# Moving columns of four up tile pairs and two down tiles in other orders

## The chip, the cores and the metric

One core of a Trainium2 chip runs the kernel. The metric is the device time of one execution in microseconds (us); 1108.68 us is the median of three runs before the change.

## The reference

The kernel computes one encoder block for 256 tokens and 16 meta tokens (`L` = 272) of width 2048 in float32: attention by two groups of heads, an output projection, and a gated MLP. The change lies in the MLP alone:

```python
def conv_glu(x, w_gate, w_up, conv_w, conv_b, w_down):
    g = x @ w_gate
    u = x @ w_up
    ...
    gc = conv_b
    for i in range(CONV_W):
        gc = gc + conv_w[i] * gp[:, i:i + L]
    return (jax.nn.silu(gc) * u) @ w_down
```

`w_gate` and `w_up` are 2048 x 5632, `w_down` is 5632 x 2048. The meta tokens are dropped at the end, so up and down need 256 tokens only.

## The kernel before

**Numbers.** Each float32 operand is split in two parts, high and low, of a type that TensorE takes faster than plain float32 (`F32R`): ScalarE writes the high part (L238), VectorE the difference (L242). A product is then three matmuls, high x high, high x low, low x high (`mm3`, L603 to L609; its matmuls are L606, L607 and L608). Weights stand still in the array as blocks of 128 x 128; activations are the moving operand, with the tokens as its columns. So one matmul writes 128 output features x 256 (or 258, or 272) tokens into a bank, and the sums over the blocks of the contraction collect in the bank.

**Weights.** Weights come from memory in pieces of up to 1024 columns (`raw`), are split into `whi` and `wlo`, and are consumed block by block: `block()` (L583) waits until a piece is split and `used()` (L590) steps on.

**Activations of the MLP.** `hl` (L629) holds the normed input, 16 blocks of 128 features, each with a high and a low half of 272 columns. `act` (L1735) holds the gated values, 44 blocks, each with a high and a low half of 256 columns that lie one behind the other, 512 columns in a row.

**Up.** The 44 tiles of 128 columns of `w_up` stand in 22 pairs. Twelve pairs (six groups of four tiles from the list `QUADS`, L48) go through another scheme with fewer products (`scheme_products`, L1924). The other ten, pairs 0, 1, 4, 7, 10, 13, 16, 17, 20 and 21, are direct: `mm_up` (L1874) calls `mm3` for each of 16 blocks and both tiles, 96 matmuls of 256 columns in a pair, into the first 256 columns of two banks. After the last block VectorE multiplies the bank with the gate (`tile_up`, L1775).

**Down.** Of the 16 tiles of `w_down`, eight go through the scheme and eight are direct. For seven of the direct ones `mm2` (L1866) is used: one matmul takes the high weights against both halves of `act` at once, 512 columns into the whole bank (L1870), and a second takes the low weights against the high half, 256 columns into the first half of the bank (L1871). `down_out` (L1842) adds the two halves of the bank. The last direct tile uses `mm3`.

**What sets the order.** The program is written by a planner (`Flow`, L111): each helper yields an engine and a cost, and the planner, with a clock for each engine, picks what can start first (`run`, L187). For an up block the cost is three times 0.445 x columns + 3 ns, for a block of `mm2` 347 ns. TensorE's order in the MLP is the list `work` (L427 on): gate and up pairs with the pieces of the scheme between them, and then down tiles with pieces of the scheme between them. `mlp_weights` (L1878) walks that list: `which` is the number of the pair or of the down tile, `k` the block in an up pair, `f` the block in a down tile.

## Time and profile before

| | |
|---|---|
| median of three runs | 1108.68 us (1108.24 to 1108.7) |
| span of the profiled execution | 1106.7 us |
| time of the profiled execution beside its span | not recorded apart; the median of the runs is 2.0 us above the span |
| instructions | 22544, of them 8414 matmuls |
| TensorE busy | 1100.6 us |
| VectorE busy | 990.8 us |
| ScalarE busy | 735.1 us |
| the four up pairs | near 390, 413, 478 and 544 us |
| the two down tiles | 871.6 to 926.7 us, with pieces of the scheme between |

The span runs from the first to the last instruction. In the groups of instructions "bank<-hl,whi 128\*128 128x256" is a matmul that reads the moving tile `hl` and the weights `whi`, 128 x 128 weights, 256 columns. Matmuls overlap, so that the durations of their records sum to more than the time they take; the distance from one start to the next is what one costs.

### The profile page before, as it was taken

What the parts mean: (1) busy time and instruction counts of PE and PEld (TensorE: products, weight loads), DVE (VectorE), ACT (ScalarE), POOL (GpSimd) and SP (SyncE); (2) the same over time, 40 slices, a digit from 0 to 9 for tenths busy, and PEclk for the clock granted to TensorE, in tenths of its full rate; (3) what the DMA queues carried; (4) which work ended last, traced back from release to release, by engine and by line L of the source; (5) the groups of instructions that cost most, each with busy time, mean ns of one, the idle gap of its engine ahead of it and who ended that gap; (6) DMA issues with size and microseconds to landing.
All of it is one profiled execution on the core that took longest, in us unless ns stands there. A gap on an engine that the chain in (4) does not pass through costs nothing.

```text
span 1106.7 us, 22544 instructions
## 1 busy us (share of the span) xinstructions
PE 1100.6 (99%) x8414; PEld 1061.8 (96%) x8414; DVE 990.8 (90%) x1837; ACT 735.1 (66%) x1470; POOL 140.0 (13%) x202
## 2 busy tenths in 40 slices
PE   9999999999999999999999999999999999999998
PEld 9999999999999999999999999999999988888888
DVE  8979888888878989999999999988988999999984
ACT  8788979798647776656666565665565565655663
POOL 3211222121433400000000000000000011100114
PEclk9999999999999999999999999999999999999999
DMA  9553434444665796657667577777688787777772
GB/s 323 199 172 124 148 127 151 139 163 134 230 188 161 207 343 229 198 181 243 224 193 230 179 248 241 238 229 244 203 275 299 260 299 250 251 258 266 281 249 77
DMA packets 72374, 239.41 MB, mean 216 GB/s; under 512 B 8136, under 2 KB 12744, under 8 KB 72264
## 3 DMA queue, kind: packets, MB, share of 16 engines
q1 hardware_dynamic: 71976, 237.69, 63.8%
q8 instruction: 66, 1.08, 0.4%
q14 instruction: 44, 0.36, 0.1%
q10 hardware_dynamic: 288, 0.27, 0.1%
HBM read 219.44 MB, written 17.83 MB: 214 GB/s over the span
## 4 chain that ended last, share of the span: by engine, by line
PE 90%; ACT 4%; DVE 3%; issue 1%; DMA 1%; POOL 0%; DVEq 0%; POOLq 0%; ACTq 0%
PE bank L278 24%; PE bank L606 18%; PE bank L607 18%; PE bank L608 18%; PE bank L1870 6%; PE bank L1871 3%; PE bank L284 2%; ACT whi L238 1%; ACT scr L238 1%; DVE wlo L242 1%; DVE scr L250 1%; DMA raw<-in_w_cq 1%; ACT qraw L238 0%; ACT bank L238 0%; DVE cols L258 0%
## 5 line engine op out<-in xcount | busy, mean ns | idle before, releaser
L238 ACT ACTIVATE whi<-raw 128x512 fp32r<-128x512 f32 (+2 forms) x479 | 358.1, 764 | 173.2 <-PE bank L607 83.5
L242 DVE TENSOR_TENSOR wlo<-raw,whi 128x512 fp32r<-128x512 f32 (+2 forms) x479 | 414.9, 885 | 43.2 <-ACT whi L238 42.1
L606 PE MATMUL bank<-hl,whi 128*128 128x258 f32 (+2 forms) x1528 | 438.5, 287 | 0.1
L607 PE MATMUL bank<-hl,whi 128*128 128x258 f32 (+2 forms) x1528 | 433.7, 284 | 0.0
L608 PE MATMUL bank<-hl,wlo 128*128 128x258 f32 (+2 forms) x1528 | 433.0, 283 | 0.2 <-DVE wlo L242 0.2
L608 PEld LDWEIGHTS bank<-hl,wlo 128*128 128x128 f32 x1528 | 290.1, 190 | 0.9 <-DVE wlo L242 0.7
L607 PEld LDWEIGHTS bank<-hl,whi 128*128 128x128 f32 x1528 | 289.6, 190 | 0.1
L606 PEld LDWEIGHTS bank<-hl,whi 128*128 128x128 f32 x1528 | 288.6, 189 | 0.5 <-ACT scr L238 0.3
L238 ACT ACTIVATE whi<-quarters 128x1024 fp32r<-128x1024 f32 x88 | 81.5, 950 | 64.8 <-PE bank L1870 46.0
L278 PE MATMUL bank<-whi,act 128*128 128x256 f32 (+1 forms) x420 | 111.5, 317 | 0.0
L1870 PE MATMUL bank<-act,whi 128*128 128x512 f32 x308 | 110.1, 397 | 0.0
L242 DVE TENSOR_TENSOR wlo<-quarters,whi 128x1024 fp32r<-128x1024 f32 x88 | 99.4, 1156 | 10.8 <-ACT whi L238 10.2
L266 POOL TENSOR_TENSOR mt<-mt,mt 128x256 f32<-128x256 f32 x7 | 6.8, 979 | 652.4 <-ACT mt L238 652.4
L1871 PE MATMUL bank<-act,wlo 128*128 128x256 f32 x308 | 86.4, 281 | 0.0
L278 PE MATMUL bank<-whi,sin 128*128 128x512 f32 (+1 forms) x272 | 83.5, 355 | 0.0
L278 PEld LDWEIGHTS bank<-whi,act 128*128 128x128 f32 x420 | 74.1, 189 | 5.7
L1870 PEld LDWEIGHTS bank<-act,whi 128*128 128x128 f32 x308 | 57.8, 188 | 13.9
L278 PE MATMUL bank<-whi,hl 128*128 128x256 f32 x288 | 66.5, 280 | 0.0
L278 PE MATMUL bank<-wlo,act 128*128 128x256 f32 (+1 forms) x210 | 66.3, 315 | 0.0
L238 ACT ACTIVATE whi<-more_raw 128x1024 fp32r<-128x1024 f32 (+2 forms) x46 | 44.1, 962 | 24.4 <-PE bank L607 9.9
L1871 PEld LDWEIGHTS bank<-act,wlo 128*128 128x128 f32 x308 | 58.1, 189 | 1.6
L278 PEld LDWEIGHTS bank<-whi,sin 128*128 128x128 f32 x272 | 49.5, 188 | 7.7
(278 smaller groups left out, 1947.9 us busy)
## 6 DMA issues: line engine op xcount, KB each, us to landing
raw<-in_w_gate SPq DMA_DIRECT2D x83, 512.0 KB, 5.0
raw<-in_w_in SPq DMA_DIRECT2D x52, 512.0 KB, 3.9
raw<-in_w_up_s SPq DMA_DIRECT2D x44, 512.0 KB, 4.9
quarters<-in_w_down_s SPq DMA_DIRECT2D x44, 512.0 KB, 6.9
raw<-in_w_up SPq DMA_DIRECT2D x34, 512.0 KB, 5.5
raw<-in_w_out SPq DMA_DIRECT2D x32, 512.0 KB, 4.0
raw<-in_w_down SPq DMA_DIRECT2D x32, 512.0 KB, 5.2
s_down<-sums SPq DMA_DIRECT2D x22, 512.0 KB, 4.1
```

The source lines that it names most:

```text
L238: nc.scalar.activation(out, in_, f, **kw)
L242: nc.vector.tensor_tensor(out, a, b, op)
L250: nc.vector.scalar_tensor_tensor(out, a, s, b, op0, op1)
L266: nc.gpsimd.tensor_tensor(out, a, b, op)
L278: nc.tensor.matmul(o, l, r, start=start, stop=stop)
L284: nc.tensor.transpose(o, i, ident[:n, :n])
L606: nc.tensor.matmul(ps, whi, xhi, start=start, stop=False)
L607: nc.tensor.matmul(ps, whi, xlo, start=False, stop=False)
L608: nc.tensor.matmul(ps, wlo, xhi, start=False, stop=stop)
L1870: nc.tensor.matmul(ps, whi, x, start=start, stop=False)
L1871: nc.tensor.matmul(ps[:, :n], wlo, x[:, 0, :], start=False, stop=stop)
```

## The change

Some matmuls read their moving columns, and write the bank, in another order. The order is a number from 0 to 7: 0 is the plain one, 7 is backwards, and 1 to 6 take runs of 2, 4, 8, 16, 32 or 64 columns in turn from the first and the second half of the columns. Source and bank take the same order, so each column still lands in its place.

In the direct up pairs with a number below 8 (0, 1, 4 and 7) the order is the block number modulo 8, for all three products. In the down tiles 0 and 1 it is the block number modulo 7, for the matmul of 512 columns alone: there the two halves are the high and the low half of `act`.

```diff
-    def mm2(ps, x, n, start, stop):
+    def mm2(ps, x, n, start, stop, order):
 
         whi, wlo = yield from block()
         yield "pe", 347
-        nc.tensor.matmul(ps, whi, x, start=start, stop=False)
+        both = x
+        if order:
+            both = x.rearrange("p i (c e) -> p c i e", e=1 << order)
+        nc.tensor.matmul(ordered(ps, order), whi, both, start=start, stop=False)
         nc.tensor.matmul(ps[:, :n], wlo, x[:, 0, :], start=False, stop=stop)
         used()
 
-    def mm_up(ps, k):
-        h = (hl[k][:, i, :SEQ] for i in range(2))
-        yield from mm3(ps[:, :SEQ], *h, k == 0, k == KC - 1)
+    def ordered(t, k):
+        if k == 0:
+            return t
+        if k == 7:
+            return t[:, ::-1]
+        e = 1 << k
+        return t.rearrange("p (h c e) -> p c h e", h=2, e=e)
+
+    def mm_up(ps, k, order):
+        h = (ordered(hl[k][:, i, :SEQ], order) for i in range(2))
+        yield from mm3(ordered(ps[:, :SEQ], order), *h, k == 0, k == KC - 1)
...
-                        yield from (mm_gate if kind == "gate" else mm_up)(pss[c], k)
+                        if kind == "gate":
+                            yield from mm_gate(pss[c], k)
+                        else:
+                            yield from mm_up(pss[c], k, k % 8 if which < 8 else 0)
...
-                        yield from mm2(ps, act[:, f], SEQ, f == 0, f == FC - 1)
+                        yield from mm2(
+                            ps, act[:, f], SEQ, f == 0, f == FC - 1, f % 7 if which < 2 else 0
+                        )
```

## The prediction

> **What bounds the kernel now.** I read the page's busy times, slices and chain first, then the waits of TensorE, then windows over the stretches that the change touches. Of the page:

> ```profile
> span 1106.7 us, 22544 instructions
> ...
> PE 1100.6 (99%) x8414; PEld 1061.8 (96%) x8414; DVE 990.8 (90%) x1837; ACT 735.1 (66%) x1470; POOL 140.0 (13%) x202
> ...
> PE   9999999999999999999999999999999999999998
> ...
> PEclk9999999999999999999999999999999999999999
> ...
> PE 90%; ACT 4%; DVE 3%; issue 1%; DMA 1%; POOL 0%; DVEq 0%; POOLq 0%; ACTq 0%
> PE bank L278 24%; PE bank L606 18%; PE bank L607 18%; PE bank L608 18%; PE bank L1870 6%; PE bank L1871 3%; PE bank L284 2%; ACT whi L238 1%; ACT scr L238 1%; DVE wlo L242 1%; DVE scr L250 1%; DMA raw<-in_w_cq 1%; ACT qraw L238 0%; ACT bank L238 0%; DVE cols L258 0%
> ```

> TensorE is busy 1100.6 of 1106.7 us at the full granted clock, and 90% of the chain that ended last is its matmuls. A busy matmul row alone does not prove that the engine is never held up, so the second view is what TensorE waited for, all of it:

> ```profile
> PE bank L698 <- DVE em L695: 1.1, 1, 1.1
> PE bank L278 <- POOL sq8r L266: 0.5, 2, 0.3
> PE bank L608 <- DVE wlo L242: 0.2, 1, 0.2
> ```

> That is 1.8 us in the whole execution. The windows over two of the four up pairs (413 and 482) and two stretches of the two down tiles (871.6 and 926.5) show the same there:

> ```profile
> core 0: us, PE busy (x) PEld busy (x) DVE busy (x) ACT busy (x) POOL busy (x), PEclk, DMA share, GB/s
> ...
> 413.00:424.00 11.00, 11.00 (x96) 11.00 (x95) 9.78 (x19) 8.17 (x14) 0.00 (x0) 1.00 0.69 235
> 482.00:490.00 8.00, 8.00 (x70) 8.00 (x69) 7.60 (x14) 3.44 (x4) 0.00 (x0) 1.00 0.45 145
> ...
> 871.60:880.00 8.40, 8.40 (x49) 7.28 (x49) 8.40 (x18) 3.77 (x6) 0.00 (x0) 1.00 0.87 302
> ...
> 926.50:930.00 3.50, 3.50 (x18) 2.90 (x17) 3.17 (x4) 3.28 (x6) 1.34 (x2) 1.00 1.01 370
> ```

> VectorE is close behind (8.40 of 8.40 us in the first down tile), but nobody on TensorE waits for it. So a nanosecond added to a matmul here is a nanosecond of the span: there is no idle time to swallow it, and the work that could have hidden it (the splits on ScalarE and VectorE, the weight loads) is work that waits for TensorE, not the other way round.

> **What a matmul costs in the stream.** The duration of a record (about 280 ns for 256 columns) is not its cost, since matmuls overlap. The cost is the step from one start to the next. The second up pair, 96 matmuls (16 blocks, 2 tiles, 3 products) and the first one behind it:

> ```profile
> 412.98 0.28 PE L606 MATMUL bank<-hl,whi 128*128 128x256 f32 x1
> ...
> 424.23 0.28 PE L608 MATMUL bank<-hl,wlo 128*128 128x256 f32 x1
> 424.34 0.28 PE L606 MATMUL bank<-hl,whi 128*128 128x258 f32 x1
> ```

> (424.34 − 412.98) / 96 = 118.3 ns for 256 columns. The first 24 blocks of the first down tile, each a matmul of 512 columns and one of 256, and then nine matmuls of 512 columns of the scheme:

> ```profile
> 871.55 0.39 PE L1870 MATMUL bank<-act,whi 128*128 128x512 f32 x1
> 871.78 0.28 PE L1871 MATMUL bank<-act,wlo 128*128 128x256 f32 x1
> ...
> 880.03 0.40 PE L278 MATMUL bank<-whi,sin 128*128 128x512 f32 x1
> ...
> 882.11 0.39 PE L1870 MATMUL bank<-act,whi 128*128 128x512 f32 x1
> ```

> A block takes (880.03 − 871.55) / 24 = 353 ns, so its wide half takes 353 − 118 = 235 ns; the nine take 2.08 / 9 = 231 ns each. From 231.1 and 118.3 follows a slope of 112.8 / 256 = **0.44 ns per column** and some 5.5 ns per instruction that do not depend on the columns.

> **The change part by part.** No instruction, wait, DMA or semaphore is added, removed or moved: the planner's costs (351 ns for the three products of an up block, 347 ns for a down block) are what they were, so it writes the same order, and no queue (SP's and POOL's included) is passed by anything. What changes is only the order in which some matmuls read their moving columns and write their bank. The groups that hold them:

> ```profile
> L1870 PE MATMUL bank<-act,whi 128*128 128x512 f32 x308 | 110.1, 397 | 0.0
> L606 PE MATMUL bank<-hl,whi 128*128 128x256 f32 x320 | 90.7, 283 | 0.0
> L607 PE MATMUL bank<-hl,whi 128*128 128x256 f32 x320 | 90.0, 281 | 0.0
> L608 PE MATMUL bank<-hl,wlo 128*128 128x256 f32 x320 | 89.8, 281 | 0.0
> ```

> Up: pairs 0, 1, 4 and 7 are the direct ones below 8, so 4 × 96 = 384 of the 960. The order is the block number modulo 8: 48 matmuls stay plain, and each of the orders 1 to 6 (runs of 2, 4, 8, 16, 32, 64 taken in turn from the two halves of 128 columns) and 7 (backwards) has 4 × 2 × 2 × 3 = 48. That is 336 altered matmuls of 256 columns. Down: two tiles of 44 blocks, order the block number modulo 7; order 1 comes 7 times in a tile and orders 2 to 6 six times each, so 14 and 5 × 12, in all 74 altered matmuls of 512 columns, which take runs in turn from the high and the low halves. The narrow matmul behind each (L1871) stays as it is.

> Loads of the stationary operand keep their addresses and are hidden as now. The instruction's fixed share stays at 5.5 ns. The unknown is the column: what it costs when its neighbour in time is not its neighbour in the buffers. The trace before has no such matmul, so I bound it. Below: two matmuls of one form with other addresses already differ in step,

> ```profile
> 482.26 0.29 PE L607 MATMUL bank<-hl,whi 128*128 128x256 f32 x1
> 482.39 0.28 PE L608 MATMUL bank<-hl,wlo 128*128 128x256 f32 x1
> ...
> 482.87 0.28 PE L606 MATMUL bank<-hl,whi 128*128 128x256 f32 x1
> 482.98 0.28 PE L607 MATMUL bank<-hl,whi 128*128 128x256 f32 x1
> ```

> 0.13 us in the first pair of rows and 0.11 in the second. If every altered matmul came down from the mean to that lower step, it would gain some 8 ns, and as much twice over where it is wide: 336 × 8 + 74 × 16 = 3.9 us gained at most. Above: the slower streams that the trace does have are the transposes and the plain float32 matmuls at the start,

> ```profile
> 489.97 1.04 PE L284 MATMUL bank<-ident,raw 128*128 128x128 f32 x8
> ...
> L284 PE MATMUL bank<-ident,raw x48: 270/273/273, 490.0 to 864.0; 128*128 128x128 f32 x48
> ...
> 1.05 3.35 PE L698 MATMUL bank<-em 128*128 128x128 f32 x14 [1.05 <-DVE em L695]
> ...
> L698 PE MATMUL bank<-em x14: 421/421/579, 1.1 to 4.0; 128*128 128x128 f32 x14
> ```

> Eight transposes take (1.04 − 0.27) / 7 = 110 ns per 128 columns, 0.86 ns a column, close to twice 0.44; fourteen plain matmuls take (3.35 − 0.42) / 13 = 225 ns, 1.76 ns a column. A stream that cannot keep its pace thus falls to about half of it or to a quarter; half is the nearest row, and I take it as the price of an order that the buffers cannot serve.

> Which orders are those? A matmul's end is already a jump, to another source tile and another bank, and costs at most those 5.5 ns. Runs of 64 make 4 such jumps in 256 columns; at 5.5 ns they would be 22 ns, at one lost column 2 ns. Runs of 2 make 128 of them, and there is no time in 0.88 ns per run for anything to be caught up. So the price should sit on the shortest runs, and I take it in two ways. At half pace for runs of 2 alone: 48 × 256 × 0.44 + 14 × 512 × 0.44 = 5.4 + 3.2 = 8.6 us. At one lost column for each run, in all orders: 48 × (128 + 64 + 32 + 16 + 8 + 4) + 14 × 256 + 12 × (128 + 64 + 32 + 16 + 8) = 18,656 runs × 0.44 ns = 8.2 us. Both come to **+8.4 us**, though they spread it differently over the orders.

> [...]

> The profiled execution's span is 1106.7 us and the median of the runs is 1108.68; the 2.0 us around the span have no part in the change. Forecast: 1108.7 + 8.4 = **1117.1 us**.

> **The rivals.** *No order costs anything:* the pairs in a run of 2 are served at pace, backwards too, or the patterns reach the engine as what they were. For it speaks that every instruction's jump is nearly free now. 1108.7 us. *Only backwards is slow:* two neighbours are always together except that they come the wrong way round, so 48 × 113 ns = 5.4 us, 1114.1 us; runs of 2 keep pace in this case. *Both are slow:* 8.6 + 5.4 = 14 us, 1122.7 us. *Every altered order falls to half pace:* 336 × 113 ns + 74 × 226 ns = 38.0 + 16.7 = 54.7 us, 1163.4 us; against it speaks that runs of 64 have so few jumps. By the quarter pace of the plain matmuls it would even be 336 × 338 ns + 74 × 676 ns = 164 us, 1272 us, which I leave out. *Faster:* the uneven steps quoted above come from addresses that collide, and reading from two places in turn avoids it. With two thirds of the bound, 2.6 us, the time is 1106.1 us. It decides from a mean gain of 5.4 ns on the 410 altered matmuls (2.2 us); the rows give no hint that order rather than address sets the step.

> **How the numbers follow.** Forecast 0.33, no cost 0.25, backwards alone 0.14, both 0.12, all at half pace 0.09, faster 0.07. About 0.2% (2.2 us) is what a measurement of this kernel can tell from no change. So slower is 0.33 + 0.14 + 0.12 + 0.09 = 0.68, same 0.25, faster 0.07. A range from 1106.5 to 1124 us holds the first four, 0.84, and leaves out the faster case and the half pace of all orders.

> **What would show it.** In the profile after, the steps in an up pair tell every order apart, since the order changes with each six matmuls: plain blocks should step at 118 ns, runs of 2 at about 230 (half pace) or 175 (lost columns, with 147 at runs of 4 and 133 at runs of 8), backwards at 118. The four pairs should then grow from 11.4 us by 1.35 us each, or by 1.3 with the loss spread. In the down tiles the wide step should be about 460 ns in one block of seven. The prediction is wrong if blocks with long runs slow as much as short ones, if backwards moves at all, or if no step moves. It is wrong in its first part if the steps grow and the span does not, which would need TensorE to have had time to spare.

## The result and the profile after

The changed kernel takes 1114.24 us (1113.76 to 1114.38) against 1108.69 us before in the same series: a ratio of 1.005 with a 95% interval of 1.0034 to 1.0066, 5.55 us more. The forecast was 8.4 us more.

The page and TensorE's waits after the change:

```profile
span 1111.9 us, 22544 instructions
...
PE 1106.0 (99%) x8414; PEld 1065.5 (96%) x8414; DVE 990.8 (89%) x1837; ACT 736.1 (66%) x1470; POOL 140.6 (13%) x202
...
PE 92%; ACT 3%; DVE 3%; issue 1%; POOL 0%; DVEq 0%; POOLq 0%; ACTq 0%
```

```profile
PE bank L698 <- DVE em L695: 1.1, 1, 1.1
PE bank L278 <- POOL sq8r L266: 0.5, 2, 0.3
```

The span has grown by 5.2 us and TensorE's busy time by 5.4 us, with the same instructions and no new wait; VectorE's busy time is what it was. So the time went into the matmuls. Which ones is read from the timeline. These are the first matmuls of blocks 1, 2, 3, 4, 7 and 8 of the second up pair; six matmuls lie from one block to the next, so a sixth of the distance is the step:

```profile
414.30 0.33 PE L606 MATMUL bank<-hl,whi 128*128 128x256 f32 x1
...
415.29 0.30 PE L606 MATMUL bank<-hl,whi 128*128 128x256 f32 x1
...
416.08 0.29 PE L606 MATMUL bank<-hl,whi 128*128 128x256 f32 x1
...
416.82 0.28 PE L606 MATMUL bank<-hl,whi 128*128 128x256 f32 x1
...
418.97 0.28 PE L606 MATMUL bank<-hl,whi 128*128 128x256 f32 x1
...
419.68 0.28 PE L606 MATMUL bank<-hl,whi 128*128 128x256 f32 x1
```

Runs of 2 (block 1) step at 0.99 / 6 = 165 ns, runs of 4 at 132, runs of 8 at 123, and the three blocks from 16 to 64 with (418.97 − 416.82) / 18 = 119 ns are where plain blocks are. Backwards (block 7) has 118 ns. In the first down tile, blocks 1 (runs of 2), 2 (runs of 4) and 3 (runs of 8), wide matmul and narrow one:

```profile
875.03 0.51 PE L1873 MATMUL bank<-act,whi 128*128 128x512 f32 x1
875.37 0.29 PE L1874 MATMUL bank<-act,wlo 128*128 128x256 f32 x1
875.49 0.41 PE L1873 MATMUL bank<-act,whi 128*128 128x512 f32 x1
875.74 0.28 PE L1874 MATMUL bank<-act,wlo 128*128 128x256 f32 x1
875.86 0.40 PE L1873 MATMUL bank<-act,whi 128*128 128x512 f32 x1
876.10 0.28 PE L1874 MATMUL bank<-act,wlo 128*128 128x256 f32 x1
```

The wide step is 340 ns for runs of 2, 250 for runs of 4 and 240 for runs of 8, where it was 235. With 48 up matmuls of each order, and 14 and 12 of the wide ones, and the means over all of them (167 and 336 ns for runs of 2, 130 and 250 for runs of 4, 123 and 240 for runs of 8): runs of 2 cost 48 × 49 + 14 × 101 ns = 3.8 us, runs of 4 0.7 us and runs of 8 0.3 us. That is 4.8 of the 5.2 us. The rest is spread over the other orders, which differ from plain by 4 ns at most, and over the narrow matmul behind each wide one with runs of 2 (127 ns in the mean, where it was 117).

### The profile page after: what moved, and what is told of

Read it like the earlier page. It is cut to its first block, busy times and chain, and to the rows that moved or that the text cites. A ratio compares the mean times of both kernels' runs of the same rounds, so it can differ in the third digit from the quotient of the medians.

```text
span 1111.9 us, 22544 instructions
## 1 busy us (share of the span) xinstructions
PE 1106.0 (99%) x8414; PEld 1065.5 (96%) x8414; DVE 990.8 (89%) x1837; ACT 736.1 (66%) x1470; POOL 140.6 (13%) x202
## 2 busy tenths in 40 slices
PE   9999999999999999999999999999999999999998
## 4 chain that ended last, share of the span: by engine, by line
PE 92%; ACT 3%; DVE 3%; issue 1%; POOL 0%; DVEq 0%; POOLq 0%; ACTq 0%
PE bank L278 24%; PE bank L606 19%; PE bank L607 19%; PE bank L608 19%; PE bank L1873 7%; PE bank L1874 3%; PE bank L284 2%; ACT whi L238 1%; DVE scr L250 1%; DVE wlo L242 1%; ACT scr L238 1%; PE bank L698 0%; DVE cols L258 0%; ACT mqr L238 0%; DVE p L246 0%
## 5 line engine op out<-in xcount | busy, mean ns | idle before, releaser
L238 ACT ACTIVATE whi<-raw 128x512 fp32r<-128x512 f32 (+2 forms) x479 | 358.3, 764 | 175.7 <-PE bank L607 87.6
L242 DVE TENSOR_TENSOR wlo<-raw,whi 128x512 fp32r<-128x512 f32 (+2 forms) x479 | 414.1, 883 | 45.5 <-ACT whi L238 44.0
L606 PE MATMUL bank<-hl,whi 128*128 128x258 f32 (+2 forms) x1528 | 439.8, 288 | 0.1
L607 PE MATMUL bank<-hl,whi 128*128 128x258 f32 (+2 forms) x1528 | 435.1, 285 | 0.0
L608 PE MATMUL bank<-hl,wlo 128*128 128x258 f32 (+2 forms) x1528 | 434.4, 284 | 0.1
L608 PEld LDWEIGHTS bank<-hl,wlo 128*128 128x128 f32 x1528 | 290.4, 190 | 0.8 <-DVE wlo L242 0.5
L607 PEld LDWEIGHTS bank<-hl,whi 128*128 128x128 f32 x1528 | 289.7, 190 | 0.1
L606 PEld LDWEIGHTS bank<-hl,whi 128*128 128x128 f32 x1528 | 288.7, 189 | 0.5 <-ACT scr L238 0.3
L238 ACT ACTIVATE whi<-quarters 128x1024 fp32r<-128x1024 f32 x88 | 81.5, 950 | 66.6 <-PE bank L1873 45.9
L278 PE MATMUL bank<-whi,act 128*128 128x256 f32 (+1 forms) x420 | 111.5, 317 | 0.0
L242 DVE TENSOR_TENSOR wlo<-quarters,whi 128x1024 fp32r<-128x1024 f32 x88 | 99.0, 1152 | 10.0 <-ACT whi L238 9.7
L266 POOL TENSOR_TENSOR mt<-mt,mt 128x256 f32<-128x256 f32 x7 | 7.4, 1050 | 656.1 <-ACT mt L238 656.1
L278 PE MATMUL bank<-whi,sin 128*128 128x512 f32 (+1 forms) x272 | 83.5, 356 | 0.0
L278 PEld LDWEIGHTS bank<-whi,act 128*128 128x128 f32 x420 | 74.1, 189 | 5.7
L278 PE MATMUL bank<-whi,hl 128*128 128x256 f32 x288 | 66.5, 280 | 0.0
L278 PE MATMUL bank<-wlo,act 128*128 128x256 f32 (+1 forms) x210 | 66.3, 316 | 0.0
L238 ACT ACTIVATE whi<-more_raw 128x1024 fp32r<-128x1024 f32 (+2 forms) x46 | 44.1, 963 | 26.0 <-PE bank L607 11.2
L278 PEld LDWEIGHTS bank<-whi,sin 128*128 128x128 f32 x272 | 49.5, 188 | 8.1 <-ACT whi L238 0.2
```

What stands on the lines that cost most here:

```text
L238: nc.scalar.activation(out, in_, f, **kw)
L242: nc.vector.tensor_tensor(out, a, b, op)
L266: nc.gpsimd.tensor_tensor(out, a, b, op)
L278: nc.tensor.matmul(o, l, r, start=start, stop=stop)
L606: nc.tensor.matmul(ps, whi, xhi, start=start, stop=False)
L607: nc.tensor.matmul(ps, whi, xlo, start=False, stop=False)
```

## The experiments

**Runs of 2 alone, and everything but them.**

```diff
-                            yield from mm_up(pss[c], k, k % 8 if which < 8 else 0)
+                            yield from mm_up(pss[c], k, 1 if k % 8 == 1 and which < 8 else 0)
...
-                            ps, act[:, f], SEQ, f == 0, f == FC - 1, f % 7 if which < 2 else 0
+                            ps, act[:, f], SEQ, f == 0, f == FC - 1, 1 if f % 7 == 1 and which < 2 else 0
```

> Only the runs of 2 are kept (48 matmuls in the four up pairs, 14 in the two down tiles); everything else is plain again. Theory one (the price sits on the runs of 2): the steps of the changed kernel, 167 against 118 ns in the up blocks and 336 against 235 ns in the down blocks, give 48 x 49 ns + 14 x 101 ns = 3.8 us, so 1112.5 us. Rival (each jump between runs costs the same, whatever the run's length): runs of 2 make 9728 of the 18656 runs, so half of the 5.5 us, 1111.5 us.

The other kernel has `k % 8 if k % 8 != 1` and `f % 7 if f % 7 != 1` in these places.

> All orders of the change but the runs of 2, backwards among them. Theory one: the rest of the steps, 11 ns at runs of 4, 4 to 5 ns at runs of 8 and 1 to 3 ns at the others, with the wide matmuls, sum to some 1.2 us, so 1109.9 us. Rival (same price for each jump): the other half of the 5.5 us, 1111.4 us.

Measured: 1112.68 us with the runs of 2 alone, ratio 1.0032 (1.0019 to 1.0044), and 1110.28 us with all the others, ratio 1.0011 (1.0002 to 1.002); before had 1109.03 us. That is 3.65 and 1.25 us, together 4.9 us. The price does sit on the runs of 2, as theory one said. The rival's equal split (2.8 and 2.8 us) does not fit: both kernels would stand at 1111.8 us, and the interval of the second ends 2.2 us above before. The 0.65 us between 4.9 and the change's 5.55 us lie inside the intervals; in the traces the up pairs and down tiles of the two kernels grow by 5.1 us together, and those of the change by 5.3 us.

**Backwards everywhere.**

```diff
-                            yield from mm_up(pss[c], k, k % 8 if which < 8 else 0)
+                            yield from mm_up(pss[c], k, 7)
...
-                            ps, act[:, f], SEQ, f == 0, f == FC - 1, f % 7 if which < 2 else 0
+                            ps, act[:, f], SEQ, f == 0, f == FC - 1, 0
```

> All 960 matmuls of all ten direct up pairs run backwards, and no other order is used. If backwards is free, as the steps of 119 ns in the changed kernel say to within some 1 ns: 1108.7 us, at most 1109.7. If it costs the half pace of my rival: 960 x 113 ns = 108 us, 1217 us.

Measured: 1108.74 us, ratio 0.9997 (0.9988 to 1.0006). Over 960 matmuls, reading and writing backwards costs nothing that this measurement can tell.

**Read and write apart.** `mm_up` gets an order for the source and one for the bank; down is plain.

```diff
+    READ = (0, 1, 1, 0, 0, 2, 2, 0, 0, 3, 3, 0, 0, 7, 0, 0)
+    WRITE = (0, 1, 0, 1, 0, 2, 0, 2, 0, 3, 0, 3, 0, 0, 7, 0)
+
-    def mm_up(ps, k, order):
-        h = (ordered(hl[k][:, i, :SEQ], order) for i in range(2))
-        yield from mm3(ordered(ps[:, :SEQ], order), *h, k == 0, k == KC - 1)
+    def mm_up(ps, k, probe):
+        r, w = (READ[k], WRITE[k]) if probe else (0, 0)
+        h = (ordered(hl[k][:, i, :SEQ], r) for i in range(2))
+        yield from mm3(ordered(ps[:, :SEQ], w), *h, k == 0, k == KC - 1)
```

> In the four up pairs read and write take orders of their own, so that the columns land in other places than they should; the values are not those of the reference. Blocks 1, 2 and 3 of a pair: runs of 2 read and written, only read, only written; blocks 5, 6 and 7 the same with runs of 4, blocks 9, 10 and 11 with runs of 8; block 13 reads backwards, block 14 writes backwards. Theory A (the price is paid where the moving columns are read): the step of block 2 is the 167 ns of block 1, block 3 is plain at 118. Theory B (paid where the bank is written): the other way round. Theory C (each jump of an address costs, on either side): both blocks 2 and 3 lie between 118 and 167, or both at 167. The same at runs of 4 with 130 ns. Blocks 13 and 14 should be at 118 in all theories.

The first matmuls of blocks 1 to 8 and 13 to 15 of its second pair:

```profile
414.24 0.33 PE L606 MATMUL bank<-hl,whi 128*128 128x256 f32 x1
...
415.23 0.34 PE L606 MATMUL bank<-hl,whi 128*128 128x256 f32 x1
...
416.22 0.30 PE L606 MATMUL bank<-hl,whi 128*128 128x256 f32 x1
...
416.95 0.28 PE L606 MATMUL bank<-hl,whi 128*128 128x256 f32 x1
...
417.66 0.29 PE L606 MATMUL bank<-hl,whi 128*128 128x256 f32 x1
...
418.44 0.29 PE L606 MATMUL bank<-hl,whi 128*128 128x256 f32 x1
...
419.20 0.29 PE L606 MATMUL bank<-hl,whi 128*128 128x256 f32 x1
...
419.92 0.28 PE L606 MATMUL bank<-hl,whi 128*128 128x256 f32 x1
...
423.53 0.28 PE L606 MATMUL bank<-hl,whi 128*128 128x256 f32 x1
...
424.23 0.28 PE L606 MATMUL bank<-hl,whi 128*128 128x256 f32 x1
...
424.96 0.28 PE L606 MATMUL bank<-hl,whi 128*128 128x256 f32 x1
```

Runs of 2 in both: 165 ns. Read alone: 165. Written alone: 122, most of what it has above 118 being in its first matmul, right behind the slow block; in the three other pairs it is 118. Runs of 4 in both and read alone: 130 and 127; written alone: 120. Runs of 8 (blocks 10 and 11, beyond these rows): 122 read alone, 119 written alone. Reading backwards steps at 117 and writing backwards at 122 (plain blocks lie between 117 and 121). **In these orders the whole price is paid where the moving columns are read**; theories B and C fall.

**What in the reading costs.** The banks are written plainly; each block of the four up pairs has a pattern of its own, and down is plain.

```diff
+    def pattern(t, k):
+        x, y = t[:, :SEQ], t[:, 2 : 2 + SEQ]
+        if k in (1, 9):
+            return x.rearrange("p (c h e) -> p c h e", h=2, e=2 if k == 1 else 4)[:, :, ::-1]
+        if k in (2, 7):
+            return x.rearrange("p (c h e) -> p h c e", h=2, e=2 if k == 2 else 4)
+        if k in (3, 12):
+            return ordered(y, 2 if k == 3 else 3)
...
+        if k in (5, 8):
+            return ordered(x, 1 if k == 5 else 2)
+        if k == 6:
+            pairs = x[:, :P].rearrange("p (c e) -> p c e", e=2)
+            return pairs.unsqueeze(2).to_broadcast((P, P // 2, 2, 2))
```

> The banks are written plainly, and in the four up pairs the moving columns are read in a pattern of each block's own; the values are not those of the reference. Theory A1 (a fetch brings four neighbouring columns that begin at a multiple of four, and what counts is how many fetches the stream needs): block 1 (the two pairs of each four swapped, 128 jumps, no more fetches than plain) at 118 ns; block 2 (the first pair of every four, then the second pairs, 128 jumps always forward) at 165, as block 5 (runs of 2 from the two halves); block 3 (runs of 4 that begin two columns late, so that each takes parts of two fetches) at 165, where block 8 (runs of 4 in place) has 130; block 12 (runs of 8 two columns late) near 142, where in place it was 123; block 6 (each pair twice, over half of the columns, each four fetched once) at 118; block 14 (every fourth pair, four rounds) at 165. Theory C (each jump costs, wherever it leads): blocks 1, 2, 5, 6 and 14 alike at 165, blocks 3 and 8 alike at 130, block 12 at 123. Blocks 7 and 13 (every second four, every second eight, two rounds) and 9 (neighbouring fours swapped) show whether the 11 ns of runs of 4 come from the distance of the two halves: then they are at 118, and at 130, 123 and 130 otherwise.

The first matmuls of blocks 1 to 10, 12 and 13 of its second pair (block 4 reads plainly, two columns late):

```profile
415.73 0.28 PE L606 MATMUL bank<-hl,whi 128*128 128x256 f32 x1
...
416.43 0.39 PE L606 MATMUL bank<-hl,whi 128*128 128x256 f32 x1
...
417.78 0.35 PE L606 MATMUL bank<-hl,whi 128*128 128x256 f32 x1
...
418.82 0.29 PE L606 MATMUL bank<-hl,whi 128*128 128x256 f32 x1
...
419.56 0.33 PE L606 MATMUL bank<-hl,whi 128*128 128x256 f32 x1
...
420.56 0.28 PE L606 MATMUL bank<-hl,whi 128*128 128x256 f32 x1
...
421.23 0.29 PE L606 MATMUL bank<-hl,whi 128*128 128x256 f32 x1
...
421.94 0.29 PE L606 MATMUL bank<-hl,whi 128*128 128x256 f32 x1
...
422.71 0.28 PE L606 MATMUL bank<-hl,whi 128*128 128x256 f32 x1
...
423.43 0.28 PE L606 MATMUL bank<-hl,whi 128*128 128x256 f32 x1
...
424.85 0.35 PE L606 MATMUL bank<-hl,whi 128*128 128x256 f32 x1
...
425.91 0.29 PE L606 MATMUL bank<-hl,whi 128*128 128x256 f32 x1
```

**The same number of jumps for all up pairs, inside the four and outside.** All 960 matmuls, read and written alike, with plain down tiles; the second kernel has `mm_up(pss[c], k, 1)` with the change's own `ordered`.

```diff
-        e = 1 << k
-        return t.rearrange("p (h c e) -> p c h e", h=2, e=e)
+        return t.rearrange("p (c h e) -> p c h e", h=2, e=2)[:, :, ::-1]
...
-                            yield from mm_up(pss[c], k, k % 8 if which < 8 else 0)
+                            yield from mm_up(pss[c], k, 1)
```

> All 960 matmuls of the ten direct up pairs read and write pairs of columns swapped within each four: 128 jumps in each, none of which leaves the four. No other order is used, the values are the reference's. Theory A1 (fetches of four count): free, 1108.7 to 1110 us. Theory C (jumps count): 960 x 48 ns = 46 us, 1155 us.

> The same 960 matmuls with runs of 2 taken in turn from the two halves, as many jumps as with the swapped pairs, each to another four. Both theories: 960 x 48 ns = 46 us, 1155 us; if TensorE did not set the time in the gate and up stage, less than that.

Measured: 1108.71 us for the swapped pairs, ratio 1.0 (0.999 to 1.0009), and 1154.68 us in one run for the two halves, 45.9 us more than before. 960 × 47 ns is 45 us: to within 1 us, each nanosecond of step is a nanosecond of the execution, over 46 us of it.

**Why 165 and not 225.** Again banks (but for block 14) and down are plain and each block of the four up pairs reads in its own pattern: runs taken in turn from 2, 4, 8, 16 or 32 places.

```diff
+    STREAMS = {1: (2, 2), 2: (4, 2), 3: (8, 2), 5: (4, 4), 6: (8, 4), 10: (4, 8), 11: (16, 2), 12: (32, 2)}
...
+        if k in STREAMS:
+            return [streams(t, *STREAMS[k]) for t in x]
...
+        if probe and k == 14:
+            out = out.rearrange("p (c h e) -> p h c e", h=2, e=2)
```

> Again banks are written plainly and each block of the four up pairs reads in a pattern of its own; the values are not those of the reference. It asks why runs of 2 from two halves take 165 ns, when pairs of every second step through the columns take 225 ns, though each jump leads to another four in both. Theory R (a four that was read a moment ago is still at hand, so coming back after one other four is cheaper): runs of 2 from 2 places (block 1) 165, from 4, 8, 16 and 32 places (blocks 2, 3, 11, 12) near 225, since more fours lie between; block 13 (each four read twice in a row, half the columns) at 112. Theory S (reads from distant places overlap, neighbouring ones do not): blocks 2 and 3 at 165 or less, block 12, whose places are 8 columns apart, nearer to 225. Blocks 7 and 8 take runs of 2 from places 272 and 256 columns apart: 165 in theory R, another time in S if distance matters. Runs of 4 and 8 from more places (blocks 5, 6, 9, 10): 118 to 130 in both. Block 14 reads plainly and writes pairs of every second step, the pattern that took 225 ns when it was read: 118 if writing is free in every order.

The first matmuls of blocks 1 to 4, 7 to 9 and 11 to 15 of its second pair:

```profile
417.21 0.33 PE L606 MATMUL bank<-hl,whi 128*128 128x256 f32 x1
...
418.20 0.42 PE L606 MATMUL bank<-hl,whi 128*128 128x256 f32 x1
...
419.57 0.42 PE L606 MATMUL bank<-hl,whi 128*128 128x256 f32 x1
...
420.94 0.32 PE L606 MATMUL bank<-hl,whi 128*128 128x256 f32 x1
...
423.27 0.33 PE L606 MATMUL bank<-hl,whi 128*128 128x256 f32 x1
...
424.25 0.34 PE L606 MATMUL bank<-hl,whi 128*128 128x256 f32 x1
...
425.25 0.30 PE L606 MATMUL bank<-hl,whi 128*128 128x256 f32 x1
...
426.72 0.38 PE L606 MATMUL bank<-hl,whi 128*128 128x256 f32 x1
...
428.02 0.41 PE L606 MATMUL bank<-hl,whi 128*128 128x256 f32 x1
...
429.42 0.29 PE L606 MATMUL bank<-hl,whi 128*128 128x256 f32 x1
...
430.10 0.28 PE L606 MATMUL bank<-hl,whi 128*128 128x256 f32 x1
...
430.83 0.28 PE L606 MATMUL bank<-hl,whi 128*128 128x256 f32 x1
```

From 2 places 165 ns; from 4, 8, 16 and 32 places 228, 228, 217 and 233 ns. Blocks 7 and 8, two places 272 and 256 columns apart, have 163 and 167: these distances do not matter. Theory R fits these steps and theory S does not: coming back to a four after one other is cheaper (163 to 167 ns) than coming back after three or more (217 to 233 ns). That a four is still at hand the first time is again a reading; no view shows it.

That it is the fours in between that count, and not the number of places, can be read from blocks 3 and 12 of the kernel before, which both read from two places. Runs of 4 two columns late come back to a four after two others: some 64 returns cost 173 − 128 = 45 ns, 0.7 ns each, as after one other ((165 − 118) / 64 = 0.7). Runs of 8 two columns late come back after three others: some 32 returns cost 177 − 123 = 54 ns, 1.7 ns each, the price from four places ((228 − 118) / 64 = 1.7). So a return after one or two other fours is the cheap one. Block 13 (fours twice in a row) has 113. Block 14 writes the bank in the pattern that costs 225 when read, at 122 ns. The longer runs from more places (blocks 5, 6, 9 and 10, not all in these rows) were expected at 118 to 130: runs of 4 from eight places have 125, from two places 272 columns apart 122, and runs of 8 from four places 123, but runs of 4 from four places have 137, which no theory here explains.

**The change's runs of 2, from four places.**

```diff
-            both = x.rearrange("p i (c e) -> p c i e", e=1 << order)
+            both = ordered(x.rearrange("p i t -> p (i t)"), order)
...
-        return t.rearrange("p (h c e) -> p c h e", h=2, e=e)
+        return t.rearrange("p (h c e) -> p c h e", h=4, e=e)
```

> As the kernel that keeps only the runs of 2 (48 matmuls in the up pairs, 14 wide ones in the down tiles), but the runs are taken in turn from four places (quarters of the columns) in place of two; bank and source in the same order, so the values are the reference's. Theory R (coming back to a four after one other is cheaper, after three it is not): the up steps go from 165 to 227 ns and the wide ones from 335 to some 450 ns, so 48 x 109 + 14 x 216 ns = 8.3 us, 1117.2 us, the price that the prediction put on runs of 2. Theory S (distant places overlap): as with two places, 1112.7 us.

Block 1 of its first down tile:

```profile
878.44 0.64 PE L1873 MATMUL bank<-act,whi 128*128 128x512 f32 x1
878.89 0.31 PE L1874 MATMUL bank<-act,wlo 128*128 128x256 f32 x1
```

This wide step is 450 ns; the mean of the 14 is 460, and the narrow matmul behind takes 142 ns in the mean where it was 117, which is most of what the expectation of 8.3 us lacks. The whole is 1117.86 us, ratio 1.0079 (1.0065 to 1.0093): 8.9 us above its own before (1109.0 us), where two places cost 3.65 us. The same runs, the same number of jumps, another number of fours in between.

## Why the prediction was right, and where it was off

**What bounds the kernel: right.** TensorE sets the time in these stages. The steps explain the span in the change (4.8 of 5.2 us from three orders), and 45 of 45.9 us in the kernel with runs of 2 in all up pairs, and no wait appeared.

**Runs of 2 carry the price: right.** 3.65 us of the two parts' 4.9 us.

**Half pace for runs of 2: the term that was mis-sized.** The prediction put 113 ns on an up matmul and 226 ns on a wide one, 8.6 us; it measured 49 and 101 ns, 3.8 us, and the second up pair grew from 11.36 to 12.21 us, by 0.85 us and not by 1.35. Half pace is a real price in other orders of reading: 225 ns for the first pairs of all fours and then the second ones, 228 ns from four places, and 8.9 us of time there. The step missed that the change comes back to each four after just one other, and such a return is cheaper (165 ns). The price was taken from the transposes, a row in which no reading order is altered. No run shows that a stream that cannot keep its pace falls to a half or a quarter of it: between 118 and 225 ns there were steps of 123, 130, 165 and 173 ns. That half pace named the right size for the other patterns is luck.

**A lost column for each run: wrong.** For runs of 2 its 175 ns lay nearer to the 167 measured than half pace did, but it gave 147 and 133 ns for runs of 4 and 8, which measured 130 and 123; and 128 jumps inside the fours cost nothing (ratio 1.0). So the two ways came to the same 8.4 us by errors in different places: one had runs of 2 too high (8.6 us for 3.8), the other mostly the longer runs (3.9 us for about 1.2). That they agreed was no support for either.

**Read and write taken together: not told apart.** The prediction spoke of neighbours "in the buffers". In the orders that were tried apart, the runs put all of it on the source. Its remark that every matmul's end is a jump to another bank is not right either: the three matmuls of `mm3` write one bank.

**The rivals.** "No order costs anything" falls with 1.0034 as the lower end of the ratio. "Only backwards" and "both" fall with 0.9997 (0.9988 to 1.0006). "Every altered order at half pace" falls with runs of 16 to 64 at 119 ns. Nor do all patterns of pairs cost alike: written alone, runs of 2 step at 118 to 122 ns; read, they step at 163 to 233 ns where the stream leaves an aligned four after two of its columns, and at 117 ns where it takes all four before it moves on (swapped pairs). "Faster" falls too: none of the orders that read each column once lowers the mean step below the plain 117 to 120 ns, backwards included. So the uneven steps of 0.11 and 0.13 us gave nothing that one of these orders could win.

What stays open is why a return after one or two other fours costs less than half of what a return after three others does (0.7 ns where that is 1.7), and why runs of 4 cost 11 ns from two halves and 19 ns from four places when every second four, or the fours swapped, cost next to none (118 and 120 ns). No run reads single columns, so whether the price goes on growing when a four is used by quarters is not shown.

## What to carry to other kernels

In these traces a matmul's moving operand (`F32R`) was read in other orders at little cost where each aligned group of four columns was used up before the stream moved on: 117 to 125 ns for 256 columns in most such orders, against 118, and 130 and 137 at worst (runs of 4 from two halves and from four places). Orders that left groups half used took 163 to 233 ns. The bank was written in every order tried apart (runs of 2, 4 and 8, pairs of every second step, backwards) at 118 to 122 ns. So where there is a choice, a permutation of these kinds is worth trying on the write side first. When a price is unknown, ask in what groups the columns might be read and how often the order comes back to one, rather than how often it jumps, and lay out a probe that gives each pattern its own block, so that one trace prices them all.

## What the runs showed that was not expected

The plain stream seems to be held by its reading itself; this is an estimate from the steps. With every pair read twice, and half the fours visited, 256 columns step at 112 ns rather than 118 (block 6 above; 113 with fours twice). Less the 5.5 ns of an instruction, if these stay the same, that is 0.416 ns per column rather than 0.44. The price of a four, worked out in the same way, agrees with this: (118.3 − 5.5) / 64 = 1.76 ns in the plain stream, where every four is visited once, and (225 − 5.5) / 128 = 1.71 ns where every four is visited twice with many others in between. The difference is 5% of a matmul, in a kernel whose TensorE is busy for 99% of the span and whose waits show nothing.
